# Turning RWKV's block inverses into rows with 32x32 TensorE products, and splitting weights on DVE alone beside RWKV

## Chip, cores and metric

One core of one Trainium2 chip. The metric is device microseconds (us) of one execution of the whole program, from the first to the last instruction of the core and what lies around it; the median of several executions counts.

## What is computed

Two layers of a mixer block on 512 latent and 256 context tokens of 2048 channels. Each layer multiplies the normalised input with one input projection (51 column tiles of 128), runs four branches on parts of the result (S5, windowed attention, RWKV-7, Hyena), gates them, and multiplies with one output projection. The change touches RWKV and the weights of the projections. RWKV's reference, cut to its recurrence:

```python
def _rwkv_step(state, inp):
    r_t, w_t, k_t, v_t, kk_t, b_t = inp
    sa = jnp.einsum('bhij,bhj->bhi', state, -kk_t)
    state = (state * w_t[:, :, None, :] + sa[..., None] * b_t[:, :, None, :]
             + v_t[..., None] * k_t[:, :, None, :])
    return state, jnp.einsum('bhij,bhj->bhi', state, r_t)

def rwkv_run(r, decay, k, v, kk, b, s0, reverse):
    ...
    s_fin, y = lax.scan(_rwkv_step, s0, (tm(r), tm(decay), tm(k), tm(v), tm(kk), tm(b)))
```

and the merge is `x + gate_x * ((y * silu(gate_pre)) @ w_out)`.

## The kernel before

**Projections.** A projection tile (128 output channels) is made of 16 products over the channels for the 512 latent tokens and, where context is needed, 16 for the 256 context tokens. Each fp32 product is three products of split operands (L1645: high x high, low x high, high x low), so one *unit* is three instructions. The weights come in 256 KB loads `wr` on SP's queue (L1629), four per tile (kq 0 to 3). `split` (L1480) makes the high part `wh` on ACT (L1484) and the low part `wl` (L1485) on DVE, for every fourth (kq 3) on POOL. Each of the two has two buffers, so a split waits until PE has used the one before the last.

**RWKV** (class `Rwkv`) takes the time steps in chunks of 64. One *block* is 4 chunks of two heads in both directions; there are 12 blocks in a layer. For each block `features` makes scores `S` (products of L340, masked on DVE in L342) and transposed operands, `invert` inverts 32 unit triangular matrices of 32x32 and joins them to 16 of 64x64 in `XT`, and `chain` runs the recurrence over 4 chunks in small steps that go from PE to DVE or ACT and back (L439, L441, L446, L448, L459, L466). `S`, `XT` and most operands have two buffers, so a block's features and inverse are made beside the chain of the block before.

**The inverse before.** The 32x32 blocks of `S` go through DRAM (`rwAd`) into `Ab`, where partition 4 u + g holds matrix u. POOL then runs 31 steps of back substitution, two instructions each (L398, L399), on `X` [128, 32, 8], in which partition 4 u + g holds columns 4 m + g of matrix u. To turn this into rows, four transfers (L401) write `X` to DRAM (`rwXd`) and one (L402) reads it back into `rwXP`. Four ACT copies (L405) put the columns in natural order into `XT`, DVE transposes two blocks (L411), and PE makes the block beside the diagonal with 16 products (L415), an ACT copy (L416), 16 more products (L421; the trace lists each product of these lines as two instructions, 32 per block) and two ACT copies (L424). The PSUM bank `mI` (one buffer) serves L415, L421 and the head norm in `finish` (L513 to L520). The chain's first use of `XT` is L446.

**Order.** The instruction order on each engine is set when the program is built, by a list scheduler with a timeline of its own; every engine then runs its list in order. RWKV is written ahead of the projections that run beside it. `Pace` ties these to it: each chain step allows some further units (`PACE`: in layer 0, 33 for the first step of a block and 3 for each later one; in layer 1, 27 and 1), and a unit beyond that stands behind the step on PE. RWKV itself is not held back by units except where they stand before it in PE's list. `self.pace` is set when RWKV has been written, and is cleared after the last gate tile of the layer; it covers 34 projection tiles of each layer.

Of the kernel before, what the change touches and what calls it, by code (L numbers as in the profile page):

```python
# [37 lines left out]
# columns of the packed RWKV parameters  # L38
# [15 lines left out]
def pack_rw(I):  # L54
    f = [cols(I["rw_mu_prev"]), cols(I["rw_mu_next"]), cols(I["rw_w0"].reshape(2, -1)), cols(I["rw_a0"].reshape(2, -1)),
         cols(I["rw_k_k"]), cols(I["rw_k_a"]), cols(I["rw_r_k"].reshape(2, -1)), cols(I["rw_ln_g"]), cols(I["rw_ln_b"])]
    p = np.concatenate(f, axis=2)
    for o in (RP["mup"], RP["mun"]):
        p[:, :, o + 12] = p[:, LORA_ORDER, o + 12]
    wa = np.stack([I["rw_w2"], I["rw_a2"]], axis=2)  # layer, direction, (w, a), row, output  # L60
    return {"rwp": p, "rwwa": np.ascontiguousarray(wa.reshape(2, 4, 32, 512))}


class K:
# [26 lines left out]
    def padded(self, lat, ctx):  # L91
        """Copies a projection tile beside zeros; its used width with the last zero excluded."""
# [8 lines left out]
    @contextmanager  # L101
    def prio(self, offset):
        """Work that goes before what was traced up to offset instructions earlier."""
        self.tc.cur_priority -= offset
        yield
        self.tc.cur_priority += offset
# [9 lines left out]
    def ring(self, shape=(128, 512)):  # L116
        """The banks beside those of the input projection, in turn."""
# [3 lines left out]
    def rms(self, y, sq, tmp, eng, eps, gate=None):  # L121
        """1 / sqrt(mean square + eps) over 4 channel tiles y, in sq (all of one width). With gate, which runs beside it: half of that, from 4 eps."""
# [19 lines left out]
class Pace:  # L142
    """Issue order on the tensor engine: units of a filling stream issue behind steps of a leading one."""
# [4 lines left out]
    def step(self, ins, allow):  # L148
        """ins leads; the units that come before it grow by allow."""
        self.n += allow  # L150
        self.steps.append((self.n, ins.ins.name))
# [18 lines left out]
class RwFeed:  # L170
    """Token shift of the RWKV projections; r, k, kk, v and the half logits kept in both orders of time."""

    def __init__(self, k, l, raw):
# [5 lines left out]
        # 1 - mu_prev - mu_next, w0 / 2, a0 / 2, k_a / 2, 1 - k_a, 2 - k_a  # L179
# [11 lines left out]
        # r, k, kk, v and tanh of the half logits (decay, a), forward and reversed  # L191
# [7 lines left out]
    def store(self, d, z, ctx):  # L199
        """z [128, 769] (latent | - | context) into d [128, 2, NT], as it is and reversed."""  # L200
# [8 lines left out]
    def feed(self, j, lat, ctx):  # L209
        """Projection tile j (r 0-3, k 4-7, v 8-11, lora 12) in lat / ctx [128, n]: token shift."""  # L210
# [17 lines left out]
        c = j % 4  # L228
# [12 lines left out]
    def logits(self, lz):  # L241
        """tanh of half the decay and a logits of all channels: (high, low, high, low) x (high, high, low, low) in one product. In 8 parts."""
# [30 lines left out]
class Rwkv:  # L273
    """Bidirectional RWKV-7 over chunks of 64 steps; both directions advance together, each in its own order of time."""
# [13 lines left out]
    def features(self, c, g):  # L288
        """Scores and transposed operands of 4 chunks of two heads."""
# [6 lines left out]
        S = t([128, 2, 4, 2, 128], "rwS", self.nbuf)  # direction, (pair, head), parity  # L296
        KU = t([128, 2, 2, 2, 2, 128], "rwKU", self.nbuf)  # direction, pair, parity, (K/B | V/U)
# [28 lines left out]
        # slots of a pair: K even | B even | B odd | K odd, in the place of k and kk  # L326
# [17 lines left out]
        # end-scaled K (natural), B (chunks of a pair exchanged)  # L344
# [25 lines left out]
    def rows(self, b):  # L370
        """Partitions of the B rows and of the K rows of chunks of parity b."""
# [5 lines left out]
    def invert(self, S, XT):  # L377
        """Transposed inverses of the unit triangular scores; column 4 m + g of matrix u on partition 4 u + g."""
# [3 lines left out]
        Xd = k.dr.tile([4, 32, 8, 32], F32, name=k.nm("rwXd"))  # L382
# [3 lines left out]
        XR, X1 = XP[:, 0], XP[:, 1]  # L386
        P1 = XR
        S8 = S.rearrange("p d u b x -> p (d u) b x")
        grp = [(b, q, self.rows(b)[0].start + 32 * q) for b in (1, 0) for q in range(2)]  # by rising row
# [10 lines left out]
        for i in range(4):  # L400
            nc.sync.dma_start(out=Xd[i].rearrange("i u (g m) -> (u g) i m", m=8), in_=X[i * 32:i * 32 + 32])  # L401
        nc.sync.dma_start(out=XR, in_=Xd.rearrange("a i u x -> (a i) u x"))  # L402
        # natural order of the columns; a row block is used from its diagonal on
        for i, (b, q, r) in enumerate(grp):
            nc.scalar.activation(XT[r:r + 32, :, 32 * q:32 * q + 32].rearrange("p u (m g) -> p u m g", g=4),  # L405
                                 XR[r:r + 32].rearrange("p u (g m) -> p u m g", g=4), AF.Copy)
        # off-diagonal block of the inverse: -X1^T A21^T X2^T
# [81 lines left out]
    def finish(self, c, Y, n0, out):  # L489
        """Head norm and bonus of the tokens from n0 on, in Y."""  # L490
# [5 lines left out]
        for a in range(n0, n0 + n, 256):  # L496
# [5 lines left out]
            # bonus: r k (2 - k_a + k_a (a forward + a backward)) summed over a head  # L502
# [73 lines left out]
def pack_s5(I):  # L576
    def st(a):  # [L,2,G,P] -> [L,128,2*G] with both halves alike
# [4 lines left out]
    lam = np.stack([st(I["s5_lam_re"]), st(I["s5_lam_im"]), stp], axis=2)  # [L,128,3,64]  # L582

    def bt(a):  # [L,2,G,P,H] -> [L,P,2G,H]
# [5 lines left out]
    bs = np.stack([np.concatenate([br, bi], 1), np.concatenate([bi, br], 1)], axis=2)  # [L,128,2,64,16]  # L590
# [7 lines left out]
class S5:  # L598
    """Bidirectional diagonal state space model over chunks of 8 tokens."""
# [7 lines left out]
    def turns(self, out, x, tmp, eng):  # L607
        """out = x - round(x)"""
# [3 lines left out]
    def prepare(self):  # L612
# [33 lines left out]
        # turns per chunk  # L646
# [6 lines left out]
        # powers 0..8 of lambda  # L653
# [18 lines left out]
        # (lambda - 1) / lam  # L672
# [15 lines left out]
        # BA = [re; im], BB = [-im; re] of the discretised input matrix  # L688
# [11 lines left out]
        # CA = [cr; -ci], CB = [-ci; -cr]  # L700
# [15 lines left out]
    def tile(self, ct, src):  # L716
        """Channel tile ct (8 groups); src [128, 768] in DRAM."""
# [6 lines left out]
        Uc = t([96, 8, 8, 16], "s5Uc")  # chunk | group, 7 - s, h  # L724
# [7 lines left out]
        U = t([128, 8, 128], "s5U")  # (7 - s, h) | group, chunks ctx, lat, ctx  # L732
# [6 lines left out]
        Yc = t([96, 8, 8, 16], "s5Uc")  # chunk | t, group, o  # L739
# [12 lines left out]
    def batch(self, g0, U, Yc):  # L752
        """Two groups, both directions."""
# [4 lines left out]
        def dg(a):  # [128, 64, ..] -> [128, 2, 2, ..]  # L758
# [7 lines left out]
        for d in range(2):  # L766
# [7 lines left out]
            # outputs at step t: forward lambda^(t+1), backward lambda^(8-t)  # L774
# [13 lines left out]
        # impulse response within a chunk: K_j[o, h] with h on partitions  # L788
# [20 lines left out]
        # drive matrices with (7 - s, h) on partitions: re | im | re  # L809
# [7 lines left out]
        # rotation tables  # L817
# [11 lines left out]
        # drives, rotated: v cos + [im; -re] sin  # L829
# [9 lines left out]
        # x: sin with the sign of [+; -]  # L839
# [6 lines left out]
        # rotated back, one chunk later, chunks in natural order lat | ctx  # L846
# [21 lines left out]
    def glu(self, outs, bg, eps):  # L868
        """Gated linear unit, then the branch norm."""
# [45 lines left out]
def hy_const(ns=(512, 256)):  # L915
    c = {}
    f = np.float32
    for n in ns:
# [6 lines left out]
        # taps: even, then odd  # L925
        h = n // 2
        ms = np.arange(n).reshape(h // 128, 128, 2).transpose(1, 2, 0)  # [128, parity, tile]
        c[f"hydec{n}"] = np.exp(-t * deltas[None, :]).astype(f)[ms].reshape(128, n // 128, 512).copy()
        # frequencies k below n / 2 (even, then odd) carry those of n - 1 - k too
# [7 lines left out]
        # [128 taps, frequency tile, cos / sin, parity, tap tile, 128]  # L937
        c[f"hykt{n}"] = kt.reshape(128, 2, 2, h // 128, h // 128, 128).transpose(0, 4, 1, 2, 3, 5).astype(f).copy()
        od = base % 2 == 1
        kk = np.concatenate([np.where(od, n - 1 - base, base), np.where(od, base, n - 1 - base)])  # even, then odd  # L940
        w = np.pi * (kk + 0.5) / n
        tau = np.arange(h)[:, None] + 0.5
        p, q = np.cos(tau * w) + np.sin(tau * w), np.cos(tau * w) - np.sin(tau * w)  # [h, n]
        # forward: a -> P even, b -> M even, b -> P odd, a -> M odd
        fw = np.stack([p[:, :h], q[:, :h], p[:, h:], q[:, h:]])  # [4, h, h]
        c[f"hyfw{n}"] = fw.reshape(4, h // 128, 128, h).transpose(2, 0, 1, 3).astype(f).copy()  # [128 t, 4, tt, k]
        c[f"hyiv{n}"] = fw.transpose(0, 2, 1).reshape(4, h // 128, 128, h).transpose(2, 0, 1, 3).astype(f).copy()  # [128 k, 4, kt, t]
# [18 lines left out]
class HyFilter:  # L966
    """Spectra of the filters. raw, split: buffers of 2 KB and their split."""
# [12 lines left out]
    def angle(self, ps, b, f, n):  # L980
        """f (ps + b) brought to the range of the sine."""
# [10 lines left out]
    def hidden(self, l, n):  # L992
        """The two layers with sines, transposed: high parts over low parts."""
# [24 lines left out]
    def tables(self, n):  # L1018
# [4 lines left out]
        self.tb = [t([128, 2, 2, 4, 128], f"hftb{i}", 1, F32R) for i in range(2)]  # frequency tile, cos / sin, (parity, taps)  # L1023
# [8 lines left out]
    def spectra(self, l, f, out):  # L1032
        """In 4 parts; appends the spectra of both orders to out."""
# [3 lines left out]
        for o in range(2):  # L1037
            # frequency tiles even then odd; [cos, sin] spectra scaled by 1 / (2 n)
# [7 lines left out]
            for s in (1, 0):  # L1046
# [4 lines left out]
                for par in range(2):  # L1051
                    S = []
                    for mt in range(h):
# [6 lines left out]
                        if par + mt == 0:  # L1060
                            # the backward filter has no tap at 0: half of sum and difference
# [29 lines left out]
class HyFeed:  # L1091
    """Convolution over 3 tokens of the projections."""
# [7 lines left out]
    def feed(self, j, lat, ctx):  # L1100
        """Projection tile j (v 0-3, x1 4-7, x2 8-11): convolution over 3 tokens."""
# [10 lines left out]
class Hyena:  # L1112
# [8 lines left out]
    def seq(self, n0, n, G):  # L1121
# [11 lines left out]
        for o in range(2):  # L1133
            # folded inputs, time on partitions
# [11 lines left out]
            # spectra P, M; products  # L1146
# [20 lines left out]
            for c in range(4):  # L1167
# [3 lines left out]
                # even P and odd M are even about the middle, the others odd  # L1171
# [16 lines left out]
    def finish(self, gates, bg, eps, put):  # L1188
        """Branch norm and gates; put takes the tiles."""
# [18 lines left out]
def att_const():  # L1208
# [5 lines left out]
    pm = np.zeros((128, 128), f)  # [source, destination]  # L1214
# [20 lines left out]
class KvFeed:  # L1235
    """RMS norm of queries and keys over heads of 64 channels."""
# [710 lines left out]
```

## Time and profile before

| | |
|---|---|
| time, median of 3 runs | 3714.03 us (3704.58 to 3720.70) |
| span of the profiled execution | 3742.2 us |
| busy: PE / DVE / ACT / POOL | 3482.5 / 2234.8 / 1491.1 / 1386.2 us |
| instructions | 63165 |
| RWKV beside projections, layer 0 | 722 to 1482 us of the span |
| RWKV beside projections, layer 1 | 2650 to 3300 us of the span |

The profiled execution is shown by its span alone, 28 us above the median of the runs without a profile. PE is TensorE's products, PEld its weight loads, DVE, ACT and POOL are VectorE, ScalarE and GpSimd, SPq is SyncE's queue, which issues the transfers. "A <- B" in a list of waits: A waited and B ended the wait. PEclk is the granted clock of TensorE as a share of 2.4 GHz; where it is 0.50 the engine runs at 1.2 GHz.

### The profile page before, as it was taken

What the parts mean: (1) busy time and instruction counts of PE and PEld (TensorE: products, weight loads), DVE (VectorE), ACT (ScalarE), POOL (GpSimd) and SP (SyncE); (2) the same over time, 40 slices, a digit from 0 to 9 for tenths busy, and PEclk for the clock granted to TensorE, in tenths of its full rate; (3) what the DMA queues carried; (4) which work ended last, traced back from release to release, by engine and by line L of the source; (5) the groups of instructions that cost most, each with busy time, mean ns of one, the idle gap of its engine ahead of it and who ended that gap; (6) DMA issues with size and microseconds to landing.
All of it is one profiled execution on the core that took longest, in us unless ns stands there. A gap on an engine that the chain in (4) does not pass through costs nothing. (4 is left out here: it accounts for less than half of the span.)

```text
span 3742.2 us, 63165 instructions
## 1 busy us (share of the span) xinstructions
PE 3482.5 (93%) x23222; PEld 2692.6 (72%) x23222; DVE 2234.8 (60%) x4239; ACT 1491.1 (40%) x2875; POOL 1386.2 (37%) x2508
## 2 busy tenths in 40 slices
PE   5897899999999999999999978999999999999999
PEld 1465777777778777788777866776776767677867
DVE  7673666546555544366667664775466565546765
ACT  3344433434344433244313454443434443435522
POOL 5642664152435242000143424663434455411031
PEclk9998999999999999999999988999988998999999
DMA  7855344554445444543633325435533433435244
GB/s 241 273 174 157 106 115 126 174 159 112 138 133 144 134 135 132 160 129 113 216 113 101 111 86 151 130 102 170 171 89 109 123 99 112 120 119 185 66 158 121
DMA packets 546737, 515.12 MB, mean 138 GB/s; under 512 B 166425, under 2 KB 392506, under 8 KB 545532
## 3 DMA queue, kind: packets, MB, share of 16 engines
q1 hardware_dynamic: 546428, 511.08, 45.2%
q8 instruction: 184, 3.01, 0.3%
q14 instruction: 125, 1.02, 0.1%
HBM read 406.59 MB, written 100.93 MB: 136 GB/s over the span
## 5 line engine op out<-in xcount | busy, mean ns | idle before, releaser
L1645 PE MATMUL pin<-hxh,wh 128*128 128x512 f32 (+1 forms) x2624 | 988.9, 377 | 10.6 <-ACT ev L267 5.0
L1645 PE MATMUL pin<-hxh,wl 128*128 128x512 f32 (+1 forms) x2624 | 946.2, 363 | 13.7 <-POOL wl L1485 10.0
L1645 PE MATMUL pin<-hxl,wh 128*128 128x512 f32 (+1 forms) x2624 | 945.8, 361 | 0.0
L1484 ACT ACTIVATE wh<-wr 128x512 fp32r<-128x512 f32 x548 | 344.4, 629 | 828.3 <-PE pin L1645 389.5
L1645 PEld LDWEIGHTS pin<-hxh,wh 128*128 128x128 f32 x2624 | 506.7, 193 | 126.7 <-issue 32.3
L1645 PEld LDWEIGHTS pin<-hxh,wl 128*128 128x128 f32 x2624 | 505.5, 193 | 96.1 <-POOL wl L1485 12.9
L1645 PEld LDWEIGHTS pin<-hxl,wh 128*128 128x128 f32 x2624 | 508.1, 194 | 73.3 <-issue 5.3
L1485 DVE TENSOR_TENSOR wl<-wr,wh 128x512 fp32r<-128x512 f32 x434 | 318.6, 734 | 306.7 <-ACT wh L1484 290.1
L1485 POOL TENSOR_TENSOR wl<-wr,wh 128x512 fp32r<-128x512 f32 x114 | 159.0, 1395 | 868.9 <-ACT wh L1484 755.5
L398 POOL TENSOR_TENSOR rwtm<-rwAb,rwX 128x60 f32<-128x60 f32 (+24 forms) x744 | 258.2, 347 | 343.9 <-DMA rwAb<-rwAd 148.1
L1735 PE MATMUL pin<-yh,wl 128*128 128x512 f32 (+1 forms) x768 | 281.5, 368 | 6.5 <-DVE wl L1485 6.4
L1735 PE MATMUL pin<-yh,wh 128*128 128x512 f32 (+1 forms) x768 | 281.8, 368 | 3.5 <-ACT yh L1711 1.3
L399 POOL TENSOR_TENSOR rwX<-rwX,rwtm 128x60 f32<-128x60 f32 (+24 forms) x744 | 263.1, 354 | 57.4
L1735 PE MATMUL pin<-yl,wh 128*128 128x512 f32 (+1 forms) x768 | 280.5, 365 | 2.3 <-DVE yl L1712 2.0
L1735 PEld LDWEIGHTS pin<-yh,wl 128*128 128x128 f32 x768 | 145.9, 190 | 32.3 <-DVE wl L1485 9.7
L1735 PEld LDWEIGHTS pin<-yh,wh 128*128 128x128 f32 x768 | 145.9, 190 | 30.1 <-ACT yh L1711 3.8
L1735 PEld LDWEIGHTS pin<-yl,wh 128*128 128x128 f32 x768 | 146.2, 190 | 26.7 <-DVE yl L1712 3.4
L1739 DVE SCALAR_TENSOR_TENSOR xt<-pin,GT,xt 128x512 f32<-128x512 f32 (+1 forms) x144 | 93.8, 656 | 87.0 <-PE pin L1735 86.7
L1542 PE MATMUL pin<-wr,cs 128*32 128x128 f32 x2048 | 119.8, 290 | 15.5 <-DMA wr<-in_wada 11.7
L448 ACT ACTIVATE rwKU<-mU 64x256 f32<-64x256 f32 x96 | 36.2, 377 | 194.4 <-PE mU L446 193.4
L466 DVE TENSOR_TENSOR rwst<-rwst,mU 64x128 f32<-64x128 f32 x160 | 45.3, 283 | 87.4 <-PE mU L459 84.6
L340 PE MATMUL mA<-rwZR,rwld 64*128 64x128 f32 x768 | 91.7, 288 | 5.5 <-DVE rwS L342 4.5
(608 smaller groups left out, 6548.7 us busy)
## 6 DMA issues: line engine op xcount, KB each, us to landing
wr<-in_win SPq DMA_DIRECT2D x408, 256.0 KB
wr<-in_wada SPq DMA_DIRECT2D x256, 256.0 KB
ada<-in_wada SPq DMA_DIRECT2D x64, 512.0 KB
wr<-in_wo SPq DMA_DIRECT2D x128, 256.0 KB
rwld<-rwF SPq DMA_DIRECT2D x20, 1024.0 KB
rwF<-ev SPq DMA_DIRECT2D x64, 256.0 KB
xt<-in_xin SPq DMA_DIRECT2D x32, 384.0 KB
rwLA<-ev SPq DMA_DIRECT2D x32, 384.0 KB
```

The lines of the kernel that those rows point to most:

```text
L340: nc.tensor.matmul(pss[:, p, b, :], kb[hr, d * 2 + p, 2 * b:2 * b + 2, :].rearrange("p b s -> p (b s)"), ZR[hr, d, :, tt * 64:tt * 64 + 64 ...
L398: E.tensor_tensor(tm, Ab[:, 0:s, s:s + 1].to_broadcast([128, s, w]), X[:, s:s + 1, m:8].to_broadcast([128, s, w]), ALU.mult)
L399: E.tensor_tensor(X[:, 0:s, m:8], X[:, 0:s, m:8], tm, ALU.subtract)
L448: nc.scalar.activation(KU[rB, :, p, b, 1, :], up[rB].rearrange("p d a b -> p d (a b)"), AF.Copy, scale=-1.0)
L466: V.tensor_tensor(new[hs, :, hs], new[hs, :, hs], sp[hs], ALU.add)
L1484: nc.scalar.activation(h, raw, AF.Copy)
L1485: (nc.gpsimd if i % 4 == 3 else nc.vector).tensor_tensor(l, raw, h.bitcast(F32), ALU.subtract)
L1542: nc.tensor.matmul(ps[32 * j:32 * j + 32, :], self.cs[:, q * 4 + j, :], w3[:, j], start=q == 0, stop=q == 3, tile_position=(0, 32 * j))
L1645: mm.append(nc.tensor.matmul(ps, w[:, c], x[:, t], start=a, stop=b))
L1735: nc.tensor.matmul(ps, w[:, c], y[:, t], start=a, stop=b)
L1739: nc.vector.scalar_tensor_tensor(x[:, t], ps, self.GT[l][:, s, j:j + 1], x[:, t], ALU.mult, ALU.add)
```

## The change

In `invert`, the four transfers to DRAM and the one back are gone. In their place PE multiplies each 32x32 part of `X` (partitions r to r + 31, one m, stationary) with a 32x32 part of the identity, at tile position (r, r): 32 products into one PSUM bank `mI`. The four ACT copies now read that bank instead of SBUF. In `split`, the low part of every fourth weight is made on POOL only while `self.pace` is not set; beside RWKV (and until the layer's last gate) DVE makes all of them.

```diff
-        Xd = k.dr.tile([4, 32, 8, 32], F32, name=k.nm("rwXd"))
...
-        XR, X1 = XP[:, 0], XP[:, 1]
-        P1 = XR
+        P1, X1 = XP[:, 0], XP[:, 1]
...
-        for i in range(4):
-            nc.sync.dma_start(out=Xd[i].rearrange("i u (g m) -> (u g) i m", m=8), in_=X[i * 32:i * 32 + 32])
-        nc.sync.dma_start(out=XR, in_=Xd.rearrange("a i u x -> (a i) u x"))
-        # natural order of the columns; a row block is used from its diagonal on
+
+        px = k.bank("mI", 1, (128, 8, 32))
+        for m in range(8):
+            for r in range(0, 128, 32):
+                nc.tensor.matmul(px[r:r + 32, m, :], X[r:r + 32, :, m], k.c["ident"][r:r + 32, r:r + 32], start=True, stop=True, tile_position=(r, r))
+
         for i, (b, q, r) in enumerate(grp):
             nc.scalar.activation(XT[r:r + 32, :, 32 * q:32 * q + 32].rearrange("p u (m g) -> p u m g", g=4),
-                                 XR[r:r + 32].rearrange("p u (g m) -> p u m g", g=4), AF.Copy)
+                                 px[r:r + 32].rearrange("p m (u g) -> p u m g", g=4), AF.Copy)
...
-        (nc.gpsimd if i % 4 == 3 else nc.vector).tensor_tensor(l, raw, h.bitcast(F32), ALU.subtract)
+        (nc.gpsimd if i % 4 == 3 and not self.pace else nc.vector).tensor_tensor(l, raw, h.bitcast(F32), ALU.subtract)
```

The rest of the diff removes comments.

## Rows read from the trace of the kernel before

**Rows 1.** The page: busy us (share of the span) and instructions by engine.

```profile
PE 3482.5 (93%) x23222; PEld 2692.6 (72%) x23222; DVE 2234.8 (60%) x4239; ACT 1491.1 (40%) x2875; POOL 1386.2 (37%) x2508
```

**Rows 2.** Windows, RWKV's two stretches: us, busy by engine, PEclk, DMA share, GB/s.

```profile
722.00:1482.00 760.00, 739.79 (x6363) 592.68 (x6361) 415.11 (x828) 302.62 (x597) 294.61 (x783) 0.98 0.48 139
2650.00:3300.00 650.00, 608.28 (x4396) 453.38 (x4396) 366.70 (x728) 270.00 (x528) 302.02 (x776) 0.90 0.41 116
```

**Rows 3.** PE's waits in layer 0's stretch: total us, times, longest.

```profile
PE mI L415 <- DVE rwXP L411: 3.7, 2, 3.5
...
PE pin L1542 <- DMA wr<-in_wada: 2.7, 2, 2.4
...
PE pin L1645 <- POOL wl L1485: 1.5, 1, 1.5
```

**Rows 4.** PE's waits in layer 1's stretch.

```profile
PE mU L439 <- DVE rwst L466: 8.9, 6, 2.4
PE mU L446 <- DVE rwBV L441: 7.1, 8, 1.4
PE mI L415 <- DVE rwXP L411: 6.1, 4, 2.6
...
PE pin L1645 <- POOL wl L1485: 3.6, 2, 3.2
```

**Rows 5.** Windows behind the three longest stops at L415.

```profile
1346.40:1356.60 10.20, 8.20 (x55) 6.61 (x56) 8.16 (x14) 5.77 (x11) 1.41 (x1) 0.50 0.28 81
2701.50:2708.30 6.80, 6.20 (x71) 5.08 (x71) 1.54 (x3) 4.46 (x12) 2.90 (x11) 0.50 0.94 299
2913.10:2919.90 6.80, 5.94 (x43) 5.07 (x44) 4.52 (x9) 4.19 (x8) 0.00 (x0) 0.50 0.35 112
```

**Rows 6.** Timeline: start, us, instruction; the end of one inverse (layer 1's last).

```profile
3278.24 0.21 POOL L399 TENSOR_TENSOR rwX<-rwX,rwtm 128x8 f32<-128x8 f32 x1
3278.47 2.98 SPq L401 DMA_DIRECT2D rwXd<-rwX  x4
3284.14 0.32 SPq L402 DMA_DIRECT2D rwXP<-rwXd  x1
3286.46 2.78 ACT L405 ACTIVATE rwXT<-rwXP 32x256 f32<-32x256 f32 x4 [2.82 <-DMA rwXP<-rwXd]
...
3289.09 1.12 PE L415 MATMUL mI<-rwXP,rwS 32*64 32x32 f32 x32 [0.28 <-DVE rwXP L411]
3290.32 0.38 ACT L416 ACTIVATE rwXP<-mI 128x256 f32<-128x256 f32 x1
...
3297.48 0.69 PE L421 MATMUL mI<-rwXT,rwXP 32*32 32x32 f32 x32
```

**Rows 7.** Splits on POOL by line, layer 0: count, ns least/median/most.

```profile
L1485 POOL TENSOR_TENSOR wl<-wr,wh x36: 1263/1292/1715, 736.9 to 1762.0; 128x512 fp32r<-128x512 f32 x36
```

**Rows 8.** Timeline of POOL: a split between two steps of an inverse.

```profile
3171.52 0.24 POOL L399 TENSOR_TENSOR rwX<-rwX,rwtm 128x24 f32<-128x24 f32 x1
3177.47 1.72 POOL L1485 TENSOR_TENSOR wl<-wr,wh 128x512 fp32r<-128x512 f32 x1 [5.72 <-ACT wh L1484]
3179.16 0.66 POOL L398 TENSOR_TENSOR rwtm<-rwAb,rwX 128x16 f32<-128x16 f32 x1
```

**Rows 9.** Timeline: a split on DVE beside steps of an inverse on POOL.

```profile
2886.40 0.68 DVE L1485 TENSOR_TENSOR wl<-wr,wh 128x512 fp32r<-128x512 f32 x1
2886.41 0.82 POOL L398 TENSOR_TENSOR rwtm<-rwAb,rwX 128x64 f32<-128x64 f32 x1
...
2887.31 0.32 POOL L399 TENSOR_TENSOR rwX<-rwX,rwtm 128x64 f32<-128x64 f32 x1
```

**Rows 10.** DVE's waits in RWKV's stretch, layer 0, then layer 1.

```profile
DVE wl L1485 <- ACT wh L1484: 47.4, 36, 6.6
...
DVE wl L1485 <- ACT wh L1484: 48.2, 29, 6.6
```

**Rows 11.** Windows of L1645 on PE between two chains, layer 1: us, busy (instructions), PEclk.

```profile
2837.60:2872.10 34.50, 23.78 (x81) 0.89 0.36 91
```

## The prediction

> **What bounds the kernel now.** I read the page first. PE is busy for 3482.5 of 3742.2 us, and no other engine for more than 60% [rows 1]. So the end is set by PE's list: its work, its stops, and the time at half clock. The change lies in two stretches, so I read these apart, as windows. In layer 0's, PE is busy for 739.8 of 760 us at a clock of 0.98: 20 us of idle time, and 4% of it, 30 us, at half clock, of which half, 15 us, would be saved at full clock. In layer 1's it is busy for 608.3 of 650 us at 0.90: 42 us idle. A mean of 0.90 over the two levels 1 and 0.5 is 20% of the time at half clock, 130 us, of which half, 65 us, would be saved at full clock [rows 2]. More than these 62 + 80 us can't be won here by shorter waits; what is added to PE's work is lost in full unless it falls into a stop.
>
> Next, PE's waits, to see what the stops are. Waits for the inverse show at L415: 3.7 us in layer 0 and 6.1 in layer 1. Waits for a split on POOL: 1.5 and 3.6 us. Most of the rest is the chain's own ping-pong, L439 and L446 behind DVE, which the change leaves as it is [rows 3, 4]. A stop costs more than itself: behind the three longest at L415 the clock is at 0.50 (1.2 GHz) for 10.2, 6.8 and 6.8 us, 23.8 us in all, in which PE is busy for most of the time [rows 5].
>
> Last, the end of one inverse in order of time. POOL ends at 3278.45, the transfers out and back take until ACT's first copy at 3286.46, so 8.0 us; L415 runs at 3289.09. But then L421 runs at 3297.48, though its operand was there at 3290.70: 6.8 us in which it stood behind other work in PE's own list [rows 6]. That is the picture of a chain that waits for PE more often than PE waits for it.
>
> **The change part by part.**
>
> *32 products more per inverse, on PE.* L421 is the nearest row: 16 products of 32x32 by 32 columns, at two tile positions, in 0.69 us [rows 6]. Twice that is 1.38 us, but the run-out of the last product stands in it twice, and other work covers it; if 32 products at four positions took the time of 16 at two, it would be 0.69 us. I take the middle, 1.0 us, times 24 inverses: +24 us. From below: 0.69 us, +17. From above: L415 has 16 products of twice the weight columns in 1.12 us [rows 6], so 32 in 2.24 us, +54. I stay near L421, since the shape is its own. PE is 97% and 94% busy in the stretches, so nearly all of it lies on the path; I hide none.
>
> A rule bears on the lower bound. L421's two positions lie in different row groups and write one bank, and the trace gives 0.69 us for them, no faster than 43 ns a product. The Trainium skill (TensorEngine Tiling (Array Packing), Gotcha 1: PSUM Pressure) says that different row tiles cannot access the same PSUM bank at the same time; all 32 new products write one bank, so by the rule four positions win nothing over two and the term is up to 24 x 1.38 = +33, while by the same page's independent tiles it would be +17.
>
> *Five transfers fewer per inverse.* The leg from POOL's end to the copies shrinks from 8.0 us to about 1.2 (the products) plus PE's queue, so the inverse is ready up to 6.8 us earlier. On PE this is worth only the stops at L415: 9.8 us [rows 3, 4], and half of the 23.8 us behind them, 12 [rows 5]: 22 us. The longest stop, 3.5 us [rows 3], is shorter than 6.8, so with PE's old order all would go. But the new products are a place of their own where PE can stand, right behind POOL, set by the scheduler's idea of POOL's time. I take -20; bounds -22 and 0 (the same stops, moved). What is late next is the chain's own stops [rows 4]. SP loses five issues and the waits before them (L401 behind POOL, L402 behind L401 [rows 6]); weight loads queued behind these come earlier. What PE waits for loads is little, 2.7 us in layer 0 [rows 3]: -2 (0 to -4).
>
> The bank `mI` is now taken from POOL's end on, and `finish` uses it too; where the head norm is still running, the products wait for it, for a few us at most in three blocks of a layer. ACT's copies keep size and count.
>
> *Splits from POOL to DVE.* 34 per layer by the code (36 rows in layer 0's time, two of them before the pace is set [rows 7]), so 68, each 1.29 us on POOL and 0.68 on DVE [rows 7, 9]. POOL's inverse loses a split of 1.3 us in nearly each phase and, now and then, a wait for ACT in the middle: in one, 5.72 us [rows 8]. PE's stops behind POOL's splits go: 5.1 us [rows 3, 4] and some half clock: -6 (bounds 0, -8). On DVE 25 splits in each stretch add 17 us to 415 and 367: 57% and 59%, no bound [rows 2]. But DVE now also waits for ACT at these: 36 and 29 such waits cost it 47.4 and 48.2 us [rows 10], 1.3 to 1.7 us each, and behind them in DVE's list stand the chain's steps (L441, L466), for which PE waits. If PE's 16 us behind these [rows 4] grow with the number of splits on DVE, by a third in layer 1, that is +5; half of it, as many waits hold no step: +3 (0 to +10).
>
> POOL's step of 128x64 takes 0.82 us beside a split on DVE, and 0.32 alone [rows 9]. The Trainium skill (SBUF — State Buffer, SBUF: two separate sides) says that a DVE operation with two SBUF inputs holds the port pair that it shares with GpSimd, and that the other blocks; the trace agrees, 0.5 us. So a moved split gives POOL's inverse 0.8 us rather than 1.3.
>
> *Sum:* +24 - 20 - 2 - 6 + 3 = -1 us, against 3742 in the profiled execution and, scaled by nothing, 3714 in the runs: **3713 us**.
>
> **The rivals.**
>
> *A, faster: the inverse's delay sets layer 1's pace.* For it: between two chains PE issues 81 instructions of L1645 [rows 11], 27 units, all that the pace allows; in the scheduler's order PE waited there. A chain needs the inverse begun two blocks earlier, so 6.8 us from the transfers and about 2 from POOL shorten a loop of two blocks by 8.8, one block by 4.4, twelve by 53 us, but not beyond PE's idle time of 42 us [rows 2]; less 12 for the products of this layer: -30. Layer 0 gives 0. Time 3684. Against it: L421 stands in PE's queue for 6.8 us [rows 6], and in this window PE's idle time is small. It decides if the chains in layer 1 follow each other by 3 us less.
>
> *B, slower: PE stands at the new products.* They come right behind POOL, whose phase differs from block to block (a split and a wait of 5.72 us in one [rows 8]), while the order is fixed. If PE comes 0.8 us too early on the mean, that is 24 x 0.8 = 19 us, and half clock behind five of these stops, at half of 6.8 us each [rows 5], 17: 3713 + 36 = 3749; twice as early gives 3785. It decides from 0.4 us per inverse on (18 us with the clock).
>
> *C, slower: the products run at L415's pace or worse,* with stationary columns 32 bytes apart: 54 instead of 24: 3743.
>
> *D: nothing on POOL changes,* if `self.pace` were not set where the splits are written; it is set before the first tile of T_Q, so I give this nothing.
>
> **How the numbers follow.** The forecast, within 0.5% (18.6 us, about what a measurement of this kernel can tell from no change): 0.44. A, 0.33, counts as faster. B 0.15 and C 0.08 count as slower. The forecast's own bounds are 3714 + 17 - 22 - 4 - 8 = 3697 and 3714 + 54 + 10 = 3778, the last only with C and with nothing won. The range takes in A to a little beyond its price, to 3672, and B and C at their first price, to 3755; it leaves out the far end of each.
>
> **What would show it.** Right: the new line with 1536 instructions on PE (32 products, each listed twice, 24 times), about 1 us per inverse; no stop at L415 above 1 us; POOL without splits in both stretches; layer 1's stretch with 35 to 45 us idle and 0.89 to 0.92 clock. Rival A: idle time below 25 us there and a shorter stretch. Rival B: PE's waits for POOL at the new line above 20 us in all. Wrong also if the chain's stops behind DVE (L439, L446) rise by over 10 us.

## The result, and the profile after

The changed kernel takes **3753.9 us** in the median (3752.0 to 3761.1), the kernel before beside it 3717.4 (3704.6 to 3723.3): a ratio of **1.010, 95% interval 1.007 to 1.013**, from four runs of each. No difference was forecast, at 3713; it is 37 us slower.

The page of after, PE, DVE, ACT and POOL, busy us (share), against [rows 1]; then the windows, against [rows 2]:

```profile
PE 3489.9 (93%) x24758; PEld 2706.7 (72%) x24758; DVE 2259.9 (60%) x4307; ACT 1458.3 (39%) x2871; POOL 1297.4 (35%) x2440
722.00:1482.00 760.00, 742.59 (x7102) 596.99 (x7101) 422.29 (x858) 284.50 (x592) 265.57 (x752) 0.98 0.45 130
2650.00:3300.00 650.00, 611.74 (x5163) 462.21 (x5156) 374.69 (x752) 256.43 (x529) 275.30 (x753) 0.92 0.39 113
```

PE is busy for 7 us more, POOL for 89 us less. PE's idle time in the two stretches is 17 and 38 us, against 20 and 42, and layer 1's clock is 0.92 against 0.90. By these rows the change has done what was hoped; yet its span is 3751.2 us. Part of the answer is that the profiled execution of before, 3742.2 us, was one of that program's longest: a second profile of it, taken in the first experiment, has 3709.6 us, and this window in it:

```profile
2650.00:3300.00 650.00, 607.45 (x4531) 452.73 (x4530) 368.57 (x743) 270.31 (x527) 305.89 (x772) 0.94 0.40 116
```

PE is busy and idle there for as long as in the first profile, within 1 us, but at a clock of 0.94 it gets 135 instructions further. Less of the window passes at half clock; it is no other kernel.

PE's waits in layer 0's stretch of after and then in layer 1's (total us, times, longest), against [rows 3, 4]:

```profile
PE mU L439 <- DVE rwst L466: 3.1, 4, 1.2
...
PE mI L402 <- POOL rwX L397: 0.8, 3, 0.3
...
PE mU L446 <- DVE rwBV L441: 11.2, 8, 3.3
PE mU L439 <- DVE rwst L466: 5.7, 4, 2.3
PE mU L446 <- ACT rwXT L424: 4.0, 1, 4.0
...
PE mI L402 <- POOL rwX L397: 3.4, 2, 2.8
```

No stop is left at L415. At the new products (L402) PE waits for POOL for 4.2 us in all. Next, the end of layer 1's last inverse in order of time (start, us, instruction), against [rows 6]:

```profile
3291.78 0.20 POOL L397 TENSOR_TENSOR rwX<-rwX,rwtm 128x8 f32<-128x8 f32 x1
3295.79 1.19 PE L402 MATMUL mI<-c_ident,rwX 32*32 32x32 f32 x64
3297.05 1.56 ACT L405 ACTIVATE rwXT<-mI 32x256 f32<-32x256 f32 x4 [0.85 <-PE mI L402]
...
3298.71 0.44 DVE L411 STREAM_TRANSPOSE rwXP<-rwXT 32x256 f32<-32x256 f32 x1
...
3302.92 1.12 PE L415 MATMUL mI<-rwXP,rwS 32*64 32x32 f32 x32
...
3309.07 0.69 PE L421 MATMUL mI<-rwXT,rwXP 32*32 32x32 f32 x32
```

This is the answer in small. The products take 1.19 us, but PE takes them up 3.8 us after POOL is done, and takes up L415 another 5.9 us after ACT's copies began, 3.8 us after its operand is ready (the end of DVE's L411). From POOL's end to L415 it is 10.9 us; with five transfers it was 10.6 [rows 6]. The operand no longer travels, it stands in PE's list.

Last, the splits: POOL's line in layer 0's stretch (two are left, ahead of the pace), and DVE's waits at its own splits in layers 0 and 1, against [rows 7, 10]:

```profile
L1485 POOL TENSOR_TENSOR wl<-wr,wh 128x512 fp32r<-128x512 f32 x2 | 2.6, 1294 | 10.4 <-ACT wh L1484 10.4
...
DVE wl L1485 <- ACT wh L1484: 79.4, 45, 6.0
...
DVE wl L1485 <- ACT wh L1484: 55.8, 37, 6.8
```

### The profile page after: what moved, and what is told of

It is laid out like the page before. It is cut to its first block, busy times and chain, and to the rows that moved or that the text cites. A ratio compares the mean times of both kernels' runs of the same rounds, so it can differ in the third digit from the quotient of the medians.

```text
span 3751.2 us, 66103 instructions
## 1 busy us (share of the span) xinstructions
PE 3489.9 (93%) x24758; PEld 2706.7 (72%) x24758; DVE 2259.9 (60%) x4307; ACT 1458.3 (39%) x2871; POOL 1297.4 (35%) x2440
## 5 line engine op out<-in xcount | busy, mean ns | idle before, releaser
L1645 PE MATMUL pin<-hxh,wh 128*128 128x512 f32 (+1 forms) x2624 | 980.6, 374 | 12.5 <-ACT ev L267 4.9
L1645 PE MATMUL pin<-hxh,wl 128*128 128x512 f32 (+1 forms) x2624 | 939.8, 361 | 8.7 <-DVE wl L1485 8.2
L1645 PE MATMUL pin<-hxl,wh 128*128 128x512 f32 (+1 forms) x2624 | 941.2, 359 | 0.0
L1645 PEld LDWEIGHTS pin<-hxh,wh 128*128 128x128 f32 x2624 | 502.5, 192 | 126.0 <-issue 33.8
L1645 PEld LDWEIGHTS pin<-hxh,wl 128*128 128x128 f32 x2624 | 501.5, 192 | 88.3 <-DVE wl L1485 9.4
L1485 DVE TENSOR_TENSOR wl<-wr,wh 128x512 fp32r<-128x512 f32 x502 | 367.9, 733 | 315.2 <-ACT wh L1484 294.4
L1645 PEld LDWEIGHTS pin<-hxl,wh 128*128 128x128 f32 x2624 | 503.8, 192 | 73.2 <-issue 6.1
L1712 POOL TENSOR_TENSOR yl<-ev,yh 128x768 fp32r<-128x768 f32 (+1 forms) x12 | 19.7, 1645 | 567.8 <-ACT yh L1711 567.8
L1542 PE MATMUL pin<-wr,cs 128*32 128x128 f32 x2048 | 119.1, 291 | 14.6 <-DMA wr<-in_wada 11.3
L1485 POOL TENSOR_TENSOR wl<-wr,wh 128x512 fp32r<-128x512 f32 x46 | 66.8, 1454 | 130.2 <-ACT wh L1484 120.2
L342 DVE TENSOR_TENSOR rwS<-mA,c_rwmask 128x512 f32<-128x512 f32 x96 | 63.8, 685 | 65.2 <-PE mA L340 64.6
```

The costliest lines, as they stand in the source:

```text
L342: V.tensor_tensor(S[:, d, h::2], pss, C["rwmask"].unsqueeze(1).unsqueeze(1).to_broadcast([128, 2, 2, 128]), ALU.mult)
L1485: (nc.gpsimd if i % 4 == 3 and not self.pace else nc.vector).tensor_tensor(l, raw, h.bitcast(F32), ALU.subtract)
L1542: nc.tensor.matmul(ps[32 * j:32 * j + 32, :], self.cs[:, q * 4 + j, :], w3[:, j], start=q == 0, stop=q == 3, tile_position=(0, 32 * j))
L1645: mm.append(nc.tensor.matmul(ps, w[:, c], x[:, t], start=a, stop=b))
L1712: (nc.gpsimd if j % 2 else nc.vector).tensor_tensor(lo[:, :n], f, h.bitcast(F32)[:, :n], ALU.subtract)
```

## The experiments

The first theory here was **P** (the products' time on PE is paid in full), with **S** (splits on DVE hold chain steps behind their wait for ACT), **A** (the inverse's delay sets the pace) and **L** (any edit brings another order of instructions, and the order moves the time) beside it. Later rivals are named where they come up.

All runs in one table. A run whose span is T at granted clock c is split into "full clock", c x T, and the rest, "half clock": half of the time spent at 1.2 GHz (means over all runs). The rest is the most that half clock can have cost, since PE stands idle in some of that time: in the profiles, 23 to 33 us of the rest are such idle time. The three right columns are worked out from the timelines of the 24 inverses of each profile: us of POOL's steps; from POOL's end to ACT's first copy; and from that copy to L415.

| kernel | ratio, 95% | full clock | half clock | POOL | to copy | to L415 |
|---|---|---|---|---|---|---|
| before | 1 | 3555 to 3563 | 153 to 161 | 28.6 | 8.9 | 3.8 |
| after | 1.0101 (1.0073 to 1.013) | 3590 | 163 | 27.0 | 6.3 | 5.8 |
| e1 before again | 1.0016 (0.999 to 1.0042) | 3560 | 160 | 28.5 | 8.4 | 3.9 |
| e2 products | 1.0035 (1.0008 to 1.0061) | 3578 | 153 | 28.8 | 5.0 | 5.6 |
| e3 splits | 1.0018 (0.9994 to 1.0042) | 3566 | 157 | 26.9 | 9.4 | 4.4 |
| e4 both | 1.0075 (1.0049 to 1.01) | 3591 | 153 | 27.1 | 5.8 | 6.0 |
| e5 products twice | 1.0020 (0.9995 to 1.0044) | 3592 | 135 | 28.5 | 6.1 | 5.8 |
| e6 turn on DVE | 0.9904 (0.9872 to 0.9936) | 3548 | 136 | 28.9 | 1.9 | 4.7 |
| e7 longer transfers | 1.0181 (1.0152 to 1.0211) | 3590 | 196 | 28.3 | 14.0 | 3.2 |
| e8 e6 + splits | 0.9968 (0.995 to 0.9985) | 3552 | 156 | 27.3 | 2.3 | 5.3 |
| e9 products + splits of layer 0 | 1.0112 (1.0087 to 1.0137) | 3592 | 164 | 28.4 | 6.1 | 5.9 |
| e10 products + splits of layer 1 | 1.0083 (1.0057 to 1.0108) | 3582 | 164 | 27.9 | 5.6 | 5.6 |
| e11 four wide products | 0.9944 (0.9925 to 0.9964) | 3565 | 130 | 28.6 | 3.6 | 5.7 |
| e12 e6 again | 0.9925 (0.9902 to 0.9947) | 3545 | 141 | 29.0 | 1.8 | 4.6 |
| e13 before, reordered | 1.0028 (1.0008 to 1.0049) | 3558 | 168 | 29.0 | 8.6 | 3.7 |
| e14 products, reordered | 1.0012 (0.999 to 1.0035) | 3571 | 149 | 28.5 | 4.8 | 5.7 |
| e15 both, reordered | 1.0060 (1.004 to 1.008) | 3579 | 160 | 27.1 | 6.1 | 5.8 |
| e16 turn on DVE, reordered | 0.9910 (0.9883 to 0.9937) | 3543 | 140 | 28.9 | 1.5 | 4.8 |
| e17 e6, half the splits on POOL | 0.9995 (0.9972 to 1.0018) | 3555 | 158 | 30.8 | 1.4 | 5.2 |
| e18 e2, half the splits on POOL | 1.0034 (1.0013 to 1.0054) | 3584 | 145 | 30.0 | 4.3 | 5.7 |

**The parts alone (e1 to e4).** e1 is the kernel before, e2 has the diff's part in `invert`, e3 its part in `split`, e4 both.

> The kernel before, unchanged, to have a profile of it on the chip of the other runs. Expected by every theory: ratio 1.000 within 0.3%. If its profiled span is near 3715 us rather than the 3742 us of the first profile, the difference of 37 us between the kernels must be looked for against this trace and not against the first; if it is near 3742, profiling itself costs the kernel before 28 us.

> The products in place of the five transfers, the splits as before (every fourth on POOL). Theory P (the products' work is paid in full by a PE that has no room, 24 times 1.2 us, and the shorter inverse wins little): ratio 1.006 to 1.010, +22 to +37 us. Theory S (the splits on DVE are what costs, as they stand ahead of the chain's steps): ratio 1.000 to 1.004.

> No weight split on POOL beside RWKV, the transfers as before. Theory P: ratio 0.998 to 1.003. Theory S: 1.005 to 1.010, +18 to +37 us, with longer waits of PE behind DVE (L439, L446) in both stretches.

> The whole change once more beside its halves on one chip: ratio 1.008 to 1.013 by every theory. If the halves add up, e2 and e3 give it as their sum; a sum that misses by over 0.4% would mean that the order of the whole list, which the scheduler makes anew for each kernel, moves the time by as much as the parts.

Neither part gains. e2 lies in S's range and e3 in P's, so neither theory holds for both; e3's interval, like that of e1, takes in no change at all. The halves add up to 0.5% and e4 is 0.75%, a miss of 0.2%, under the 0.4% that was asked for the order. e4 has the instructions of after in the same order on PE, DVE, ACT and POOL; it lies just below the expected 1.008, and its interval and that of after overlap. At full clock the products add 18 us and the splits 6 alone, 13 beside the products.

**The products twice (e5).** The edit is against e2.

```diff
-        for m in range(8):
+        for m in [*range(8), *range(8)]:
```

> As e2_products_only, but each of the 32 products is made twice into the same place (64 per inverse). Theory P (PE has no room, the products' time is paid in full): the second set costs its own PE time, 24 times about 1.0 us, so ratio 1.008 to 1.013, some 0.65% above e2's 1.0035. Rival L (the products fall into PE's idle time, and the loss comes from the new order or from clock): within 0.25% of e2, 1.002 to 1.006.

That is some 24 us more of PE's work than in e2, and no more time: at full clock it costs 14 us, and 18 come back at the clock. So P, as "paid in full", fails on the whole time; at full clock it holds for the larger part.

**The turn off PE (e6), and the transfers longer (e7).** Both change the delay, with no work added to PE. e6 leaves out PE and the transfers: DVE's block transpose does all 32 products in one instruction (the edit is against e2). e7 sends the rows through DRAM once more (against before).

```diff
-        px = k.bank("mI", 1, (128, 8, 32))
-        ...
+        XQ = t([128, 8, 32], "rwXQ")
+        nc.vector.transpose(XQ.rearrange("p m s -> p (m s)"), X.rearrange("p i m -> p m i"))
...
-                                 px[r:r + 32].rearrange("p m (u g) -> p u m g", g=4), AF.Copy)
+                                 XQ[r:r + 32].rearrange("p m (u g) -> p u m g", g=4), AF.Copy)
```

```diff
         nc.sync.dma_start(out=XR, in_=Xd.rearrange("a i u x -> (a i) u x"))
+        Xe = k.dr.tile([128, 8, 32], F32, name=k.nm("rwXe"))
+        nc.sync.dma_start(out=Xe, in_=XR)
+        nc.sync.dma_start(out=XR, in_=Xe)
```

> No transfers and no products: one 32x32-block transpose on DVE (128 x 256, about 0.45 us) turns the columns to rows; splits as before. The inverse is ready as early as with the products, PE has no work more. Theory P: the loss of e2 is gone, ratio 0.996 to 1.001. Rival A (the inverse's delay sets layer 1's pace, and the products only hide it): 0.985 to 0.994. Rival L (the loss comes from the new order): still 1.002 to 1.006.

> The kernel before with one more round trip through DRAM behind the one it has, some 4 to 5 us more delay in each inverse, no work for PE, ACT, DVE or POOL. Theory P (the inverse's delay is mostly covered by units on PE): ratio 0.999 to 1.004. Rival A: layer 1's twelve blocks are longer by half of 4.5 us each, +27 us or more, 1.006 to 1.012.

The delay has a price in both directions, as theory A has it, and e7's lies above A's range. e7's inverse comes to its copies 5.1 us later than before's, and costs 65 us, 37 of them at half clock; e6's comes 7 us earlier and gains 37 (means of the runs). PE's waits of e7 show the delay where the prediction looked for it, in layer 0 and then in layer 1 (L418 and L1545 are L415 and L1542 there), against 3.7 and 6.1 us [rows 3, 4]:

```profile
PE mI L418 <- DVE rwXP L414: 13.7, 7, 3.8
PE pin L1545 <- DMA wr<-in_wada: 10.1, 6, 4.0
...
PE mI L418 <- DVE rwXP L414: 14.1, 9, 3.1
```

But e7's loss does not lie where rival A put the price. From the first product of L446 to that of the next block, e7 takes 64.3 us in layer 0, where the two profiles of before have 59.7 and 59.8, and 54.0 in layer 1, where they have 53.8 and 52.1: some 50 us of its profile are lost in layer 0, for which A had nothing. Nor is all of it the inverse's: in layer 0 PE waits for weight loads for 10.1 us, against 2.7 [rows 3], and these loads share SP's queue with the two new transfers, at which the queue waits for 43 us in this stretch.

e6's kernel (run again as e12, 3688 us, as expected if 0.9904 holds, and 9 us below e11) beats before and after. In e12's profile, DVE's instruction by source (count, ns least/median/most), and the end of layer 1's last inverse (L413 is L415):

```profile
L400 DVE STREAM_TRANSPOSE rwXQ<-rwX x24: 595/673/716, 789.2 to 3228.4; 128x256 f32<-128x256 f32 x24
...
3225.84 0.21 POOL L398 TENSOR_TENSOR rwX<-rwX,rwtm 128x8 f32<-128x8 f32 x1
3228.43 0.68 DVE L400 STREAM_TRANSPOSE rwXQ<-rwX 128x256 f32<-128x256 f32 x1
3229.14 1.72 ACT L403 ACTIVATE rwXT<-rwXQ 32x256 f32<-32x256 f32 x4 [1.43 <-DVE rwXQ L400]
...
3233.27 1.12 PE L413 MATMUL mI<-rwXP,rwS 32*64 32x32 f32 x32
```

It is 7.2 us from POOL's end to the products of L413, where after has 10.9. In the mean over 24 inverses DVE, busy for 61% of e12's span, takes the turn up 1.0 us behind POOL, and PE, busy for 93% of after's, takes up its products 3.9 us behind it; and 0.67 us of DVE adds nothing to PE's work.

**The turn on DVE, with the splits moved (e8).** The diff's part in `split` on top of e6.

> e6 with no weight split on POOL beside RWKV. If the splits on DVE cost by themselves (3 to 10 us, as between e1 and e3): 0.15 to 0.3% above e6. If the difference of e3 was chance: as e6 within 0.2%.

It costs 24 us beside e6 (more than the 0.15 to 0.3% expected), and 16 by the ratio of e12. The inverse is not to blame: POOL has 1.6 us less, and from POOL's start to L415 it is 34.9 us, as in e6 and e12 (35.5, 35.4). At full clock it is 4 to 7 us, the rest is at half clock.

**Where the splits cost, and the products' share again (e9 to e12).** e9 and e10 move the splits of one layer only, beside the products (`self.pl` is the layer; the line is e9's, against e4, and e10 has 1 for 0). e11 puts four products of the identity with 256 columns each in place of the 32 (against e2), so the turn itself is left out.

```diff
-        (nc.gpsimd if i % 4 == 3 and not self.pace else nc.vector).tensor_tensor(l, raw, h.bitcast(F32), ALU.subtract)
+        (nc.gpsimd if i % 4 == 3 and not (self.pace and self.pl == 0) else nc.vector).tensor_tensor(l, raw, h.bitcast(F32), ALU.subtract)
```

```diff
-        for m in range(8):
-            for r in range(0, 128, 32):
-                nc.tensor.matmul(px[r:r + 32, m, :], X[r:r + 32, :, m], k.c["ident"][r:r + 32, r:r + 32], start=True, stop=True, tile_position=(r, r))
+        for r in range(0, 128, 32):
+            nc.tensor.matmul(px[r:r + 32], k.c["ident"][r:r + 32, r:r + 32], X[r:r + 32].rearrange("p i m -> p m i"), start=True, stop=True, tile_position=(r, r))
```

> The products, and POOL without splits beside layer 0's RWKV alone. The products alone stood at 1.0035 of before, with both layers' splits moved at 1.0075, so the moved splits cost 0.4%, 15 us. Theory S (DVE's waits for ACT at the splits hold the chain's steps; in layer 0 these waits went from 47 to 79 us, in layer 1 from 48 to 56): the cost lies in layer 0, so 1.006 to 1.008 here. Rival G (the cost lies at layer 1's start, where one 9 us stop of PE shows when both layers' splits are moved): 1.002 to 1.0045 here. Rival L (no place of its own, any new order of the instructions moves the time by such an amount): anything from 0.998 to 1.010, and this and the next don't add up.

> The products, and POOL without splits beside layer 1's RWKV alone. Theory S: 1.003 to 1.0045, as the products alone. Rival G: 1.006 to 1.008. Rival L: anything from 0.998 to 1.010; the two layers' shares over 1.0035 don't add up to 0.4%.

> In place of 32 products of 32x32 by 32 columns, four of 32x32 by 256 columns with the identity stationary, at the same place: the turn itself is left out, so the values are others. About half the time on PE (8 of 32 loads' worth of instructions, the same columns). Theory P (what the products cost is PE's time, about 1 us per inverse): 12 us less than with the 32, so 1.000 (0.998 to 1.002). Rival Q (it is their place in PE's list, behind POOL, that costs): as with the 32, 1.002 to 1.006. Rival A alone (PE's part is free, all that counts is the earlier inverse): 0.988 to 0.994, as with the turn on DVE.

> The turn on DVE (one 32x32 block transpose of 128 x 256), POOL keeps its splits, beside the run above on one chip. If the 0.9904 holds: 0.987 to 0.994, and 7 to 12 us or more below the four wide products by theory P. If it was the chance of one chip: 0.996 to 1.002.

Over the products, layer 0's splits cost 0.8%, layer 1's 0.5%, and both 0.4%: they don't add up, so neither S nor G holds as put, and L is alive, though e9 lies above its range too. One piece of it shows in a stretch that neither edit touches, layer 1's start. PE's longest wait there in after, and the window; then the window in e2, which has no such wait:

```profile
PE pin L235 <- ACT ev L232: 8.2, 1, 8.2
...
2163.00:2630.00 467.00, 399.47 (x2514) 317.61 (x2515) 292.99 (x562) 206.52 (x383) 211.44 (x319) 0.93 0.43 124
```

```profile
2166.00:2641.00 475.00, 417.98 (x2622) 331.74 (x2622) 296.19 (x571) 215.07 (x394) 213.58 (x322) 0.94 0.44 129
```

The stretch runs from the end of layer 0's output projection to RWKV's first product of layer 1. 108 PE instructions have moved out of it, 18.5 us of work, but it is only 8 us shorter. The wait, 8.2 us each time, is in the profiles of after, e4, e8, e9 and e17, not in those of e2, e10, e14, e15 and e18. In e15 the splits cost as much without it.

e11 was to take half of PE's time away and didn't: 1.10 us per inverse, nearly as long as the 32. It is nevertheless some 35 us faster than e2, which no theory of PE's time explains (0.9944 lies below P's and Q's bounds, just above A's). Its inverse comes to the copies 1.4 us sooner; 13 us of the gain are at full clock, 23 at half clock.

**The order by itself (e13 to e16).** Four kernels with one neutral edit: the first two projection tiles beside RWKV change places.

```diff
-        for c in (4, 5, 0, 1, 2, 3):
+        for c in (5, 4, 0, 1, 2, 3):
```

> The kernel before with one neutral edit: of the first two projection tiles beside RWKV, values come before keys (5, 4 for 4, 5). Work, buffers and counts stay; the instructions of every engine come in another order from there on. Theory N (the order alone moves the time): off 1 by more than 0.3% to either side. Theory M (the times follow from the change's own parts): 0.997 to 1.003.

> The products alone, in the neutral other order. The products alone stood at 1.0035 of before in the old order. Theory M: 0.1 to 0.6% above the kernel before in the other order. Theory N: a difference to it of another sign, or over 0.8%.

> The whole change, in the neutral other order. It stood at 1.0075 and 1.010 of before in the old order. Theory M (products' PE time and the splits on DVE): 0.5 to 1.2% above the kernel before in the other order. Theory N: under 0.3%, or over 1.4%.

> The turn on DVE, POOL keeps its splits, in the neutral other order. It stood at 0.9904 and 0.9925 in the old order. Theory M (the earlier inverse is worth some 30 us when PE does nothing for it): 0.6 to 1.2% below the kernel before in the other order. Theory N: under 0.3% below it, or above it.

The order alone moves the kernel before by 0.28%, at the edge of M's range. Against the kernel before in the same order, the products stand at +0.35% and -0.16%, the whole change at +0.75% (+1.0% in its first runs) and +0.3%, the DVE turn at -1.0% (-0.75% in e12) and -1.2%. So N holds for the products, by the sign; but -0.16% is within the intervals of e13 and e14, and what is shown is that the order moves their share by about 0.5%, as much as the share itself. M holds for the DVE turn. The whole change is slower in both orders, in the second by an amount at the edge between the two.

**More splits on POOL (e17, e18).** The opposite dose: beside RWKV every second split on POOL.

```diff
-        (nc.gpsimd if i % 4 == 3 else nc.vector).tensor_tensor(l, raw, h.bitcast(F32), ALU.subtract)
+        (nc.gpsimd if i % 4 == 3 or (self.pace and i % 4 == 1) else nc.vector).tensor_tensor(l, raw, h.bitcast(F32), ALU.subtract)
```

> The turn on DVE, and beside RWKV every second split on POOL, not every fourth (34 more per layer). With none on POOL it stood at 0.9968, with every fourth at 0.9904, 0.9925 and, in the other order, 0.991. Theory S (a split on DVE holds the chain's steps behind its wait for ACT): a further gain, 0.984 to 0.989. Rival T (a split on POOL holds the inverse, 1.3 us and its own wait for ACT; one of four was the optimum): 0.992 to 0.998.

> The 32 products, and beside RWKV every second split on POOL. With none on POOL the products stood at 1.0075, with every fourth at 1.0035. Theory S: 0.997 to 1.001. Rival T: 1.005 to 1.011. If this run and the one before it go to different sides, the order decides.

No dose law: with the DVE turn, none, a quarter and half of the splits on POOL give 0.997, 0.991 and 0.9995; with the products 1.0075, 1.0035 and 1.0034. In the first the time goes T's way, beyond T's range; in the second neither holds. That DVE's waits at the splits are the price is thus not shown.

## Why the prediction was wrong, step by step

**The products' time, +24: right.** The last inverse's 1.19 us [the timeline above] less the run-out of the last product, 0.22, is 0.97 us, times 24 is +23. PE's work over a whole profile, with time at half clock counted half, agrees: 3351 and 3352 us in e2 and e14 against 3327 to 3331 in three profiles of before (the first, e1's and e13's). How much of it lies on the path is less sure: of e5's second set, 24 us of work, 14 came out at full clock.

**The transfers, -20: a step that failed.** "The leg from POOL's end to the copies shrinks from 8.0 us to about 1.2 (the products) plus PE's queue": the queue was named and got no number. It is 3.9 us in the mean over 24 inverses of after, and the products take 2.05 us from first to last, not 1.19, since in some blocks steps of the chain stand among them in PE's list. So the leg is 6.3 us, not 1.2. The next leg took back what was left. ACT's copies, which the prediction left as they were, take 1.55 us out of PSUM instead of 2.75, so L415's operand is ready 8.6 us behind POOL's end, against 11.4 and 10.9 in the two profiles of before. But PE comes to L415 3.5 us behind its operand, not 1.3, and from POOL's end to L415 it is 12.1 us, against 12.7 and 12.3. Counted from POOL's first step, the inverse was to come 8.8 us sooner by the prediction's rival A (6.8, and 2 from POOL); it came to L415 1.6 to 2.2 us sooner, about what POOL's own part gave. From POOL's end to L415 it is 10.0 us in layer 0, against 12.1 and 12.4, and 14.2 in layer 1, against 13.2 and 12.1: where the clock and the idle time had left something to win, L415 came no earlier. The stops at L415 did vanish, as forecast, because PE now came to L415 late. At full clock e2 shows +18 where PE's work alone is +23: this leaves 5 for the stops, and 11 in the other order, of the 10 and the 2 for loads that were forecast. Of the 12 us of half clock e2 got 2 back (153 us against 156 beside it), e14 6 against before and 19 against e13, and after lost 7.

**What a shorter leg is worth: undersized, in the other direction.** The prediction capped it at 22 us. e6, e12 and e16 have the leg near the forecast (1.5 to 1.9 us) and no work on PE, and gain 28 to 37 us beside their runs of before: 14 to 17 at full clock and 11 to 23 at half clock. Rival A put the worth of it at 42 us before the products and asked for chains that follow each other by 3 us less in layer 1. Between the first products of L446 of one block and the next it is 53.8 and 52.1 us in the profiles of before, 54.2 in after, and 51.1 and 50.6 with the turn on DVE (53.5 and 49.7 in the other order). So layer 1's pace does follow an earlier inverse, by 1 to 4 us per block, and the whole change had none of it. That it follows a later one is not shown: e7's 54.0 us is within 2 us of before.

**The splits, -3: the other step that failed, wrong in sign.** POOL's part went as said: its steps take 27.0 us instead of 28.6, near the forecast 2, and PE's stops behind POOL's splits are gone. (The 0.32 us that [rows 9] gives for a step alone is that of L399; L398 alone takes 0.29 us in the trace, so the reading stands.) The price was sought at L439 and L446, but these stops come to 16.9 us, against 16.0 [rows 4] and 17.7 in the two profiles of before, so none of the forecast +3 shows there; DVE's waits at L1485 did rise, by 32 and 8 us [rows 10]. In six pairs of runs that differ in splits alone (e3 and before, e4, e9 and e10 and e2, e8 and e6, e15 and e14) moving them cost 8 to 25 us by the means, 4 to 14 of it at full clock, and in none did it gain; e3's 8 us alone would not be clear of noise.

By whole times this is the larger miss. In the old order the products came to +13 us (e2) where +24 - 20 - 2 = +2 was forecast, and the splits beside them to +15 (e4 over e2) where -3 was. In the other order the products came to -6 (e14 over e13) and the splits to +18 (e15 over e14). By the intervals each of these is known to some 10 to 14 us. The first miss changes sign with the order, the second does not.

**The sum again, from the runs.** At full clock, after is some 30 us above before: +23 for the products, -5 for the stops, +12 for the splits (3590 against 3578 in e2). Some 7 us more are lost at half clock. That makes 37. The -5 and the +12 are what is left between runs, not sums of waits, and the other order gives other shares.

**The signs.** All that were named as "right" came true: 1536 instructions at about 1 us, no stop at L415, POOL without splits but for two in each stretch, 38 us idle and a clock of 0.92 in layer 1; rival B's sign (20 us of waits for POOL) did not come. They were signs of PE's work and stops, and none measured when the operand arrived. B had the place right, the new products, and the side wrong: PE did not stand at them, they stood behind PE. The new line in the whole profile of after (count, busy us, mean ns, PE's idle time before it):

```profile
L402 PE MATMUL mI<-c_ident,rwX 32*32 32x32 f32 x1536 | 31.4, 224 | 4.2 <-POOL rwX L397 4.1
```

**What stays open.** Why moved splits cost what they cost: not through the inverse (e8), not by a dose law (e17, e18), in part with a wait at layer 1's start that comes and goes with the order. And why e5 and e11, with as much PE work as e2 or more, lose 20 us less at half clock; the order may be all of it, but no run shows that.

## What to carry to other kernels

A stop that disappears from a list of waits is not time won: follow the operand from its producer's end to its consumer's start, since a consumer that the busiest engine reaches late shows no wait at all. Work handed to that engine costs its duration and its place in the list; give it to an engine with slack (here one DVE instruction, about 1% faster than before in both orders). And before a part of 0.3% is believed, reorder something neutral: that alone moved this kernel by as much.

## What the runs showed of the hardware

**Four tile positions, one PSUM bank.** The end of one inverse of e11, and its products by source (count, ns least/median/most):

```profile
3244.07 1.10 PE L401 MATMUL mI<-rwX,c_ident 32*32 32x256 f32 x8
...
L401 PE MATMUL mI<-rwX,c_ident x192: 619/628/637, 798.8 to 3244.5; 32*32 32x256 f32 x192
```

Eight instructions of 0.63 us each (four products, listed twice) are done in 1.10 us: the first four start within 20 ns of each other, the other four 0.45 us behind them. So the four positions run beside each other, though all write one bank. The Trainium skill (TensorEngine Tiling (Array Packing), Gotcha 1: PSUM Pressure) says that different row tiles cannot access the same bank at the same time; here the measurement differs, and it decides. The 32 small ones still take 1.19 us [the timeline above], about the same for the same columns.

**One program, many clocks.** The kernel before took 3698 to 3743 us beside these experiments. Two profiles of it, 32.6 us apart in span, differ by 2.5 us in PE's idle time between its first and last product, and by 34 us in half of the time at 1.2 GHz: a single profile's clock is no measure of a change of 1%.
